# Weight blocks at other addresses and a 256/288 cut of the tokens in a one-core decoder layer

## The chip, the core and the metric

The kernel runs on one core of one Trainium2 chip. The core has a matmul engine (TensorE, "PE" in the profile, with its weight loads in a row of their own, "PEld"), a vector engine (VectorE, "DVE"), an activation engine (ScalarE, "ACT"), a general engine (GpSimd, "POOL") and a queue engine (SyncE, "SP") that issues all transfers of this kernel. They run side by side and wait for each other by semaphores. On-chip memory has 128 partitions; matmul results go to a second memory (PSUM) in banks of 512 fp32 numbers a partition. The metric is the device time of one execution in microseconds; smaller is better.

## The reference

One decoder layer, for a prompt of 512 tokens and a group of 8 x 4 sample tokens, all in fp32, model width 1024:

```python
h = _rmsnorm(x, norm_in)
proj = jnp.matmul(h, w_in)                     # 15,896 columns, split among four branches and gates
y_a = rmsnorm(ssd(...) * silu(z_ssd))          # A: Mamba-2 scan
y_b = s5(u) -> gelu -> * sigmoid(y @ glu_w) * silu(z_s5)   # B: diagonal complex SSM, 64 groups of 16
y_c = rmsnorm(sigmoid(o) * mlstm(q, k, v)) * silu(z_ml)    # C: matrix memory, 4 heads x 256
y_d = attention(q, mem_k, mem_v) * silu(z_xa)  # D: 256 memory tokens
down = jnp.einsum('btkw,kwd->btkd', branches, w_down)
merged = jnp.sum(sigmoid(gate_raw + b_gate) * down, axis=2)
x = x + jnp.matmul(merged, w_out)              # then a last RMSNorm
```

States of the three recurrent branches, and the memory's keys and values, are outputs too.

## The kernel before

The 512 prompt tokens and 32 sample tokens form one row of `NT` = 544 columns. Features lie on partitions: an activation such as h is a tile of 128 partitions by 8 row blocks (`NK`) by 544 tokens, so a row block is 544 x 4 = 2176 bytes of a partition. Each fp32 number is held as two rounded parts, hi and lo; `xh`, `xl` hold the normed input, `oh`, `ol` the current branch's output.

Nearly all projections go through one function, `unit` (line 166). It computes 128 output features for all 544 tokens: `load` fetches a 1024 x 128 block of weights (512 KB, three buffers `raw`), ACT casts it to `whi` (line 177), DVE subtracts for `wlo` (line 178, recorded at the helper's line 64), and PE runs, for each of 8 row blocks, hi x hi, hi x lo and lo x hi, each on two halves of 272 tokens (line 188): 48 matmuls, each with its own weight load of 128 x 128. `whi`, `wlo` and the result `pu` have two buffers each. In `pu` half a starts at the start of bank a. There are 165 such units; 16 further ones (`w_mem_kv`) have one part of 256 tokens, the memory's, 24 matmuls each, with token blocks of 1024 bytes. Two early units already cut at 256 and 288 (`ECUT`, line 242), because their first part starts before all tokens are there. The last product (line 1644) is written out by itself, also in parts of 288 and 256.

The work is staged: norm and transposes; cross-attention with the memory's units between; the S5 branch (lines 687 to 888); its GLU; the SSD branch; mLSTM; the last gate units; the last product. Generators such as `gate_down` are stepped between the steps of a branch, so that units fill TensorE while other engines work. The tile framework orders the instructions of each engine ahead of time by a simulated schedule: an instruction can be placed ahead of an earlier one of the program if that one still waits. On the chip each engine keeps that order.

The S5 branch runs over eight blocks f. `s5_in` runs a permuted unit, writes its result to DRAM (`ud`, line 709) and reads it back in another order into `U` (line 710, two buffers). `s5_mats` builds the block's matrices, `s5_scan` multiplies U (line 779) and scans on DVE and POOL (its first product on DVE writes `gr`, line 787), `s5_y` multiplies U a second time (line 834), and its result goes through DRAM again (`yd`, `yt`, lines 839 and 840) to `s5_out`. `s5_in` runs up to two blocks ahead. Smaller buffers that matter here: `kbt` (line 432, transposed keys of the sample group), `fo` (line 1217, a final state on its way out), `sqm` (line 1459), `yvx` (line 679).

Of the kernel before, what the change touches and what calls it, by code (L numbers as in the profile page):

```python
# [8 lines left out]
F32 = mybir.dt.float32  # L9
F32R = mybir.dt.float32r  # L10
# [6 lines left out]
P = 128  # L17
# [3 lines left out]
TS = 32  # L21
NT = TP + TS
HALF = NT // 2
NK = D // P
EPS = 1e-6
# [9 lines left out]
def hybrid_kernel(ctx: ExitStack, tc: tile.TileContext, I, O):  # L35
# [127 lines left out]
    def halves(t):  # L163
        return t.rearrange("p (a t) -> p a t", a=2)

    def unit(w, op, perm=False, raw=None, cols=HALF, nh=2, apart=False, later=False, cuts=None):

        if raw is None:
            raw = load(w)
        hi = wp.tile([P, NK, P], F32R, name="whi", tag="whi")  # L170
        lo = wp.tile([P, NK, P], F32R, name="wlo", tag="wlo")
        rv, hv, lv = raw, hi, lo
        if perm:
            rv = raw.rearrange("p k (g c) -> p k g c", c=16)
            hv = hi.rearrange("p k (c g) -> p k g c", g=8)
            lv = lo.rearrange("p k (c g) -> p k g c", g=8)
        S.copy(hv, rv)  # L177
        tt(V, lv, rv, hv.bitcast(F32), SUB)
        ps = psg.tile([P, 2, 512], F32, name="pu", tag="pu")
        xhi, xlo = op  # L180

        def part(rng):
            for k in range(NK):
                for wt, xt, first in ((hi, xhi, k == 0), (hi, xlo, False), (lo, xhi, False)):
                    last = k == NK - 1 and wt is lo
                    for a in rng:
                        c0, c1 = cuts[a] if cuts else (a * cols, (a + 1) * cols)
                        T.matmul(ps[:, a, 0:c1 - c0], wt[:, k, :], xt[:, k, c0:c1], start=first, stop=last)  # L188
        if later:
            return ps, part  # L190
        for rng in ([(a,) for a in range(nh)] if apart else (range(nh),)):
            part(rng)
        return ps
# [17 lines left out]
    def gate_down(k, first=False, ahead=2, place=None):  # L211
        gq = []

        def gate(i):
            pg = unit(wcols(C_G + k * D + i * P), x2)
            g = place(i) if place else ev.tile([P, NT], F32, name="gt", tag="gt")
            S.activation(halves(g), pg[:, :, 0:HALF], AF.Tanh, scale=0.5, bias=colh("b_gate", k * NK + i))
            gq.append(g)

        for i in range(ahead):  # L220
            gate(i)
            yield
        for i in range(NK):
            g = gq[i]
            pd = unit(I["w_down"][0, k][:, i * P:(i + 1) * P], o2)
            if first:
                stt(halves(merged[:, i, :]), halves(g), 1.0, pd[:, :, 0:HALF], ADD, MUL)
            else:
                stt(halves(g), halves(g), 1.0, pd[:, :, 0:HALF], ADD, MUL)
# [11 lines left out]
    early = []  # L241
    EC, NE, ECUT = 1, 2, ((0, 256), (256, NT))
    for c in range(5):
# [7 lines left out]
        if c < 4:  # L251
# [8 lines left out]
            if c == EC:  # L260
                for i in range(NE):
                    early.append(unit(None, x2, raw=qraw[i], later=True, cuts=ECUT))
                    early[i][1]((0,))
# [60 lines left out]
    for i in range(3):  # L324
        if i < NE:
            pu, part = early[i]
            part((1,))
            for a, (c0, c1) in enumerate(ECUT):
                S.copy(oh[:, i, c0:c1], pu[:, a, 0:c1 - c0])
                tt(V, ol[:, i, c0:c1], pu[:, a, 0:c1 - c0], oh[:, i, c0:c1].bitcast(F32), SUB)  # L330
            V.tensor_copy(qs[:, i, :], pu[:, 1, 256:288])
        else:
            pu = unit(wcols(C_QX + i * P), x2, raw=qraw[i])
            S.copy(halves(oh[:, i, :]), pu[:, :, 0:HALF])
            tt(V, halves(ol[:, i, :]), pu[:, :, 0:HALF], halves(oh[:, i, :].bitcast(F32)), SUB)
            V.tensor_copy(qs[:, i, :], pu[:, 1, 240:272])
    xmc = ExitStack()
# [25 lines left out]
    for i in range(3, NK):  # L363
        pu = unit(wcols(C_QX + i * P), x2)
        S.copy(halves(oh[:, i, :]), pu[:, :, 0:HALF])
        tt(V, halves(ol[:, i, :]), pu[:, :, 0:HALF], halves(oh[:, i, :].bitcast(F32)), SUB)
        V.tensor_copy(qs[:, i, :], pu[:, 1, 240:272])
    def mem_units():
        for i in range(16):
            pu = unit(I["w_mem_kv"][0][:, i * P:(i + 1) * P], (mh, mlo), cols=256, nh=1)  # L370
            src = xm.tile([P, 256], F32, name="vfm", tag="vfm", bufs=2)
            S.copy(src, pu[:, 0, 0:256])
            if i < 8:
# [48 lines left out]
    for b in range(NB):  # L422
# [274 lines left out]
    def s5_in(f):  # L697
# [6 lines left out]
        us = pu[:, 1, 240:272].rearrange("p (b t) -> p t b", t=4)  # L704
# [198 lines left out]
    def glu(gl):  # L903
# [4 lines left out]
        for i in range(NK):  # L908
            pg = unit(I["s5_glu_w"][0][:, i * P:(i + 1) * P], o2)
            sg = gl.tile([P, NT], F32, name="sg", tag="sg")  # L910
            S.activation(halves(sg), pg[:, :, 0:HALF], AF.Tanh, scale=0.5, bias=colh("s5_glu_b", i))
            stt(sg, sg, 1.0, zq[i], ADD, MUL)
# [6 lines left out]
    with tc.tile_pool(name="sd", bufs=1, side="right", reuse_waits="tile") as sd:  # L919
# [43 lines left out]
        def rows():  # L963
            with tc.tile_pool(name="sx", bufs=1, side="left", reuse_waits="tile") as sx:
# [9 lines left out]
                sp = sx.tile([96, NT], F32, name="sp", tag="sp")  # L974
                V.tensor_scalar(halves(X), pu[0:96, :, 0:HALF], bcol[:, 0:1], bcol[:, 1:2], ADD, MUL)
                irow = sx.tile([4, NT], F32, name="irow", tag="irow")
                S.activation(halves(irow), pu[32:36, :, 0:HALF], AF.Identity, bias=bcol[32:36, 0:1])
                yield
# [149 lines left out]
        def conv(ct):  # L1128
# [3 lines left out]
            G.memset(R[:, 0:3], 0.0)  # L1132
            S.copy(halves(R[:, 3:3 + NT]), pu[:, :, 0:HALF])
            sv = R[:, 515:571].rearrange("p (b s) -> p b s", s=7)
            V.tensor_copy(sv[:, :, 3:7], pu[:, 1, 240:272].rearrange("p (b t) -> p b t", t=4))
            V.tensor_copy(sv[:, :, 0:3], cvs[:, ct, :].rearrange("p (b t) -> p b t", t=3))
# [33 lines left out]
        for j in range(8):  # L1170
# [45 lines left out]
            T.transpose(pf[:, 0:P], SS[:, 3, :], ident)  # L1216
            fo = sr.tile([P, P], F32, name="fo", tag="fo")
            S.copy(fo, pf[:, 0:P])
# [36 lines left out]
        def ml_qkv(h, dst):  # L1255
            for t, keep, c0, sc in zip(dst, (qs, ks, vs), (C_Q, C_K, C_V), (1.0, 1.0 / 16.0, 1.0)):
                for dt in range(2):
                    pu = unit(wcols(c0 + h * 256 + dt * P), x2)
                    S.mul(halves(t[:, dt]), pu[:, :, 0:HALF], sc)
                    if dt == 0:  # L1260
# [128 lines left out]
    with tc.tile_pool(name="mlr", bufs=1, side="right", reuse_waits="tile") as mr:  # L1389
        for h in range(4):  # L1390
# [67 lines left out]
            to = mr.tile([P, 2, NT], F32, name="to", tag="to")  # L1458
            sq = mr.tile([P, TP], F32, name="sqm", tag="sqm")
            for dt in range(2):  # L1460
                pu = unit(wcols(C_O + h * 256 + dt * P), x2)
                S.activation(halves(to[:, dt]), pu[:, :, 0:HALF], AF.Tanh, scale=0.5)
                V.tensor_copy(os_[:, 2 * h + dt, :], to[:, dt, TP:NT])
# [266 lines left out]
```

## Time and profile before

| | us |
|---|---|
| median of 3 runs | 1526.18 |
| lowest and highest run | 1525.82, 1528.65 |
| the profiled execution | 1523.98 |
| its span, first to last instruction | 1522.2 |
| matmuls of line 188: busy in the span | 1121.18 |
| mean granted TensorE clock | 0.973 of full speed |

The profile is one execution on the chip. Its page gives, for each engine, the busy time, its share of the span and the count of instructions; then the span in 40 slices; then the chain of work that ended last, followed back from the last instruction. A view by stretches gives, for each stretch of the span, the busy time of PE, PEld, DVE, ACT and POOL (with counts), the granted clock, the share of time in which the DMA engines were busy, and GB/s. A timeline lists instructions by start time: start, duration, engine, line, operation, output tile <- input tiles, shapes, count of like instructions merged into the row, all in microseconds. Matmuls are pipelined: each takes some 0.28 to 0.30 us from start to end, but the next one starts long before that. What a stream of them costs is the distance between starts.

### The profile page before, as it was taken

The page shows a single profiled execution, that of the slowest core. Times are in us where ns is not written, and L with a number is a line of the kernel's source. Part 1 is how long each engine was busy: PE and PEld are TensorE (multiplying, and loading weights), DVE is VectorE, ACT ScalarE, POOL GpSimd, SP SyncE. Part 2 cuts the span into 40 slices and gives each one's busy share as a digit, 9 for nine tenths or more (in the row PEclk, how much of TensorE's full clock was granted, in tenths as well). Part 3 has the DMA queues.
Part 4 walks back from the last instruction along what each step waited for, and adds up shares of the span by engine and source line. Part 5 has one row for each costly group of instructions (what it writes and reads, how often), then busy time and mean ns, then how long its engine had stood idle before and what let it go on. Part 6 is the DMA issues. An engine that isn't in the chain of part 4 may idle for free.

```text
span 1522.2 us, 28087 instructions
## 1 busy us (share of the span) xinstructions
PE 1446.7 (95%) x11505; PEld 1364.3 (90%) x11505; DVE 925.6 (61%) x1810; ACT 485.5 (32%) x825; POOL 349.2 (23%) x527
## 2 busy tenths in 40 slices
PE   6999999789879899999999999999999999899997
PEld 6988888678768899999999989999999998789997
DVE  6355487898778768486787644354343456554543
ACT  5244333222222333243333322243332332113332
POOL 2000133766465201101232322100000011110222
PEclk9999999999789999999999999999999999999999
DMA  8577362435334333322222355222222225673341
GB/s 200 159 215 221 99 200 59 106 93 126 82 92 108 84 100 82 86 78 81 74 73 74 97 167 146 70 70 77 77 78 74 79 82 176 197 218 113 94 146 59
DMA packets 288034, 171.75 MB, mean 113 GB/s; under 512 B 36934, under 2 KB 278922, under 8 KB 287907
## 3 DMA queue, kind: packets, MB, share of 16 engines
q1 hardware_dynamic: 287906, 169.97, 40.4%
q8 instruction: 90, 1.47, 0.4%
q14 instruction: 38, 0.30, 0.1%
HBM read 145.35 MB, written 24.60 MB: 112 GB/s over the span
## 4 chain that ended last, share of the span: by engine, by line
PE 63%; DVE 10%; DMA 4%; issue 3%; POOL 2%; ACT 1%; SPq 0%; POOLq 0%; ACTq 0%; DVEq 0%
PE pu L188 48%; PE pu L1644 3%; DVE wlo L64 2%; DVE hs L64 1%; DMA raw<-in_w_out_dram 1%; DMA yd<-yj 1%; PE pacc L1557 1%; DVE bbs L752 1%; DVE cm L67 1%; PE pcu L1442 1%; DMA out_dram<-cb 1%; PE pn L1436 1%; PE py L834 1%; PE py L835 1%; DMA cb<-in_state_mlstm_c_dram 1%
## 5 line engine op out<-in xcount | busy, mean ns | idle before, releaser
L188 PE MATMUL pu<-xh,whi 128*128 128x272 f32 (+1 forms) x2000 | 432.8, 294 | 1.3 <-DVE uf L706 1.1
L188 PE MATMUL pu<-xh,wlo 128*128 128x272 f32 (+1 forms) x2000 | 428.9, 293 | 0.0
L188 PE MATMUL pu<-xl,whi 128*128 128x272 f32 (+1 forms) x2000 | 428.2, 292 | 0.6 <-DVE xl L64 0.6
L64 DVE TENSOR_TENSOR wlo<-raw,whi 128x1024 fp32r<-128x1024 f32 x181 | 251.5, 1390 | 226.3 <-ACT whi L177 221.1
L177 ACT CAST whi<-raw 128x1024 fp32r<-128x1024 f32 x181 | 198.9, 1099 | 502.6 <-PE pu L188 373.1
L188 PEld LDWEIGHTS pu<-xh,whi 128*128 128x128 f32 x2000 | 322.1, 191 | 8.3 <-issue 6.2
L188 PEld LDWEIGHTS pu<-xl,whi 128*128 128x128 f32 x2000 | 322.2, 192 | 5.6 <-issue 4.5
L188 PEld LDWEIGHTS pu<-xh,wlo 128*128 128x128 f32 x2000 | 320.2, 191 | 5.5 <-issue 5.1
L188 PE MATMUL pu<-oh,wlo 128*128 128x272 f32 x640 | 135.6, 292 | 6.0 <-DVE wlo L64 6.0
L188 PE MATMUL pu<-oh,whi 128*128 128x272 f32 x640 | 136.5, 292 | 0.0
L188 PE MATMUL pu<-ol,whi 128*128 128x272 f32 x640 | 136.4, 292 | 0.0
L188 PEld LDWEIGHTS pu<-oh,wlo 128*128 128x128 f32 x640 | 102.0, 191 | 7.7 <-DVE wlo L64 6.6
L188 PEld LDWEIGHTS pu<-ol,whi 128*128 128x128 f32 x640 | 102.7, 191 | 1.6 <-issue 1.5
L188 PEld LDWEIGHTS pu<-oh,whi 128*128 128x128 f32 x640 | 102.9, 191 | 1.0 <-issue 0.8
L64 POOL TENSOR_TENSOR merged<-merged,gt 128x544 f32<-128x544 f32 x18 | 29.1, 1616 | 142.0 <-DVE gt L67 141.9
L67 DVE SCALAR_TENSOR_TENSOR cb<-cb,dcm,pcn 128x257 f32<-128x257 f32 x64 | 28.5, 478 | 26.4 <-PE pcn L1563 26.1
L834 PE MATMUL py<-U,tp 128*128 128x72 f32 x128 | 28.3, 307 | 13.8 <-DVE hn L64 7.1
L67 DVE SCALAR_TENSOR_TENSOR cc<-cc,dcm,pcu 128x257 f32<-128x257 f32 x24 | 11.5, 478 | 44.4 <-PE pcu L1442 44.4
L188 PE MATMUL pu<-mh,whi 128*128 128x256 f32 x128 | 37.7, 294 | 0.1
L188 PE MATMUL pu<-mlo,whi 128*128 128x256 f32 x128 | 37.7, 295 | 0.0
L64 POOL TENSOR_TENSOR SS<-SS,dec 128x128 f32<-128x128 f32 x24 | 19.5, 814 | 77.6 <-DVE SS L1210 49.8
L188 PE MATMUL pu<-mh,wlo 128*128 128x256 f32 x128 | 36.2, 283 | 0.0
(641 smaller groups left out, 2297.7 us busy)
## 6 DMA issues: line engine op xcount, KB each, us to landing
raw<-in_w_in_dram SPq DMA_DIRECT2D x124, 512.0 KB
raw<-in_w_down_dram SPq DMA_DIRECT2D x32, 512.0 KB
kb<-in_cache_mem_k_dram SPq DMA_DIRECT2D x8, 1024.0 KB
raw<-in_w_mem_kv_dram SPq DMA_DIRECT2D x16, 512.0 KB
vb<-in_cache_mem_v_dram SPq DMA_DIRECT2D x16, 512.0 KB
cb<-in_state_mlstm_c_dram SPq DMA_DIRECT2D x16, 512.0 KB
out_dram<-cb SPq DMA_DIRECT2D x16, 512.0 KB
tp<-kd SPq DMA_DIRECT2D x8, 512.0 KB
```

The costliest lines, as they stand in the source:

```text
L64: eng.tensor_tensor(out, a, b, op)
L67: V.scalar_tensor_tensor(out, a, s, b, op0, op1)
L177: S.copy(hv, rv)
L188: T.matmul(ps[:, a, 0:c1 - c0], wt[:, k, :], xt[:, k, c0:c1], start=first, stop=last)
L752: V.tensor_copy(bbs[64 * ri:64 * ri + 64, :, g2, :], src[64 * g2:64 * g2 + 64, gs])
L834: T.matmul(o, tp[:, g, :], U[:, g, 0:72], start=True, stop=False)
L835: T.matmul(o, cm[:, g, 1:9, :].rearrange("p l c -> p (l c)"), hs_[:, g, 0:72], start=False, stop=True)
L1436: T.matmul(p2[:, 0:257], qh[:, dt, sl], cc[:, dt, 0:257], start=dt == 0, stop=dt == 1)
L1442: T.matmul(p3[:, 0:CE], k_[:, dt * P:(dt + 1) * P], v_, start=j == 0, stop=j == 2)
L1557: T.matmul(pacc[32 * h:32 * h + 32, 0:257], qm[:, 2 * h + dt, :], cbs_[h // 2][:, 2 * (h % 2) + dt, 0:257], start=b == 0 and dt == 0, stop ...
L1644: T.matmul(pu, wt[:, k, :], mk[:, t0:t1], start=k == 0 and j == 0, stop=k == NK - 1 and j == 2)
```

## The change

Every two-part unit now cuts the tokens at 256, so its parts have 256 and 288 columns. In `pu` the first part ends at the border of the two banks and the second begins there, so that the 544 results are one run; every reader of `pu` reads that run in place of two halves.

The weight tiles `whi` and `wlo` are larger (1128 numbers a partition in place of 1024). The even row blocks lie first, the odd ones 128 bytes further on than they would without a gap, and the matmuls take the blocks in the order 0, 2, 4, 6, 1, 3, 5, 7. The start of the `whi` part moves by 32 bytes from unit to unit, through six places; that of the `wlo` part moves every six units. Units of the memory have no gap between even and odd blocks but the same order and starts. The permuted units of S5 cast and subtract even and odd blocks separately.

To make room, `U` of the S5 branch has one buffer in place of two, `kbt` five in place of six, `fo` one in place of two; `sqm` shares the place of `Wl`, and `yvx` that of `qxs`.

```diff
+CUTS = ((0, 256), (256, NT))
+KS = (0, 2, 4, 6, 1, 3, 5, 7)
+WS = 4 * 128 + 32
...
+    turn = iter(range(1000))
...
-        hi = wp.tile([P, NK, P], F32R, name="whi", tag="whi")
-        lo = wp.tile([P, NK, P], F32R, name="wlo", tag="wlo")
-        rv, hv, lv = raw, hi, lo
+        u = next(turn)
+        hi, lo = (wp.tile([P, 2 * WS + 40], F32R, name=n, tag=n)[:, 8 * o:8 * o + 2 * WS]
+                  for n, o in (("whi", u % 6), ("wlo", (u // 6) % 6)))
+        if nh == 2:
+
+            hi, lo = (t.rearrange("p (o q) -> p o q", o=2)[:, :, 0:4 * P] for t in (hi, lo))
+        else:
+            hi, lo = (t[:, 0:NK * P].rearrange("p (o q) -> p o q", o=2) for t in (hi, lo))
+        rv = raw.rearrange("p (k o) c -> p o k c", o=2)
         if perm:
...
+            parts = [tuple(t[:, o].rearrange("p k (g c) -> p k g c", c=16) if t is rv else t[:, o].rearrange("p (k c g) -> p k g c", k=4, g=8)
+                      for t in (hi, lo, rv)) for o in range(2)]
+        else:
+            parts = [(hi.rearrange("p o (k c) -> p o k c", k=4), lo.rearrange("p o (k c) -> p o k c", k=4), rv)]
+        for hv, lv, rv in parts:
+            S.copy(hv, rv)
+            tt(V, lv, rv, hv.bitcast(F32), SUB)
...
-            for k in range(NK):
-                for wt, xt, first in ((hi, xhi, k == 0), (hi, xlo, False), (lo, xhi, False)):
-                    last = k == NK - 1 and wt is lo
+            for s, k in enumerate(KS):
+                for wt, xt, first in ((hi, xhi, s == 0), (hi, xlo, False), (lo, xhi, False)):
+                    last = s == NK - 1 and wt is lo
                     for a in rng:
-                        c0, c1 = cuts[a] if cuts else (a * cols, (a + 1) * cols)
-                        T.matmul(ps[:, a, 0:c1 - c0], wt[:, k, :], xt[:, k, c0:c1], start=first, stop=last)
+                        c0, c1 = CUTS[a]
+                        T.matmul(ps[:, a, 256 * (1 - a):256 * (1 - a) + c1 - c0], wt[:, s // 4, (s % 4) * P:(s % 4 + 1) * P],
+                                 xt[:, k, c0:c1], start=first, stop=last)
+
+        po = ps.rearrange("p a t -> p (a t)")[:, 256:256 + NT] if nh == 2 else ps[:, 0, 256:512]
...
-        S.activation(halves(z), pu[:, :, 0:HALF], AF.Tanh, scale=0.5)
-        stt(halves(z), halves(z), 1.0, pu[:, :, 0:HALF], ADD, MUL)
+        S.activation(z, pu, AF.Tanh, scale=0.5)
+        stt(z, z, 1.0, pu, ADD, MUL)
...
-            kt_ = xk.tile([P, 2, 256], F32, name="kbt", tag="kbt", bufs=6)
+            kt_ = xk.tile([P, 2, 256], F32, name="kbt", tag="kbt", bufs=5)
...
-    yv = xv.tile([P, 8, TS], F32, name="yvx", tag="yvx", bufs=1)
+    yv = xa.tile([P, 8, TS], F32, name="yvx", tag="qxs")
...
-        S.copy(uf[:, :, 8:42], pu[:, 0, 0:272].rearrange("p (k s) -> p s k", s=8))
-        S.copy(uf[:, :, 42:72], pu[:, 1, 0:240].rearrange("p (k s) -> p s k", s=8))
+        S.copy(uf[:, :, 8:72], pu[:, 0:TP].rearrange("p (k s) -> p s k", s=8))
...
-        U = s5r.tile([P, 8, NV], F32, name="U", tag="U", bufs=2)
+        U = s5r.tile([P, 8, NV], F32, name="U", tag="U", bufs=1)
...
-            fo = sr.tile([P, P], F32, name="fo", tag="fo")
+            fo = sr.tile([P, P], F32, name="fo", tag="fo", bufs=1)
...
-            sq = mr.tile([P, TP], F32, name="sqm", tag="sqm")
+            sq = mr.tile([P, TP], F32, name="sqm", tag="Wl")
```

More of the change, by code (lines that the diff above doesn't have):

```diff
@@ L160, in hybrid_kernel, with unit @@
     x2, o2 = (xh, xl), (oh, ol)
+    turn = iter(range(1000))
     ev = ctx.enter_context(tc.tile_pool(name="ev", bufs=2))
-    def halves(t):
-        return t.rearrange("p (a t) -> p a t", a=2)
-    def unit(w, op, perm=False, raw=None, cols=HALF, nh=2, apart=False, later=False, cuts=None):
+    def unit(w, op, perm=False, raw=None, nh=2, later=False):
         if raw is None:
             raw = load(w)
-        hi = wp.tile([P, NK, P], F32R, name="whi", tag="whi")
-        lo = wp.tile([P, NK, P], F32R, name="wlo", tag="wlo")
-        rv, hv, lv = raw, hi, lo
-        if perm:
[L174 to L178, printed above, removed]
+        u = next(turn)
[6 more added lines that the diff above has]
+        rv = raw.rearrange("p (k o) c -> p o k c", o=2)
+        if perm:
+            parts = [tuple(t[:, o].rearrange("p k (g c) -> p k g c", c=16) if t is rv else t[:, o].rearrange("p (k c g) -> p k g c", k=4, g=8)
[5 more added lines that the diff above has]
+            tt(V, lv, rv, hv.bitcast(F32), SUB)
         ps = psg.tile([P, 2, 512], F32, name="pu", tag="pu")
@@ L182, in part @@
         def part(rng):
-            for k in range(NK):
-                for wt, xt, first in ((hi, xhi, k == 0), (hi, xlo, False), (lo, xhi, False)):
-                    last = k == NK - 1 and wt is lo
+            for s, k in enumerate(KS):
+                for wt, xt, first in ((hi, xhi, s == 0), (hi, xlo, False), (lo, xhi, False)):
+                    last = s == NK - 1 and wt is lo
                     for a in rng:
-                        c0, c1 = cuts[a] if cuts else (a * cols, (a + 1) * cols)
-                        T.matmul(ps[:, a, 0:c1 - c0], wt[:, k, :], xt[:, k, c0:c1], start=first, stop=last)
+                        c0, c1 = CUTS[a]
+                        T.matmul(ps[:, a, 256 * (1 - a):256 * (1 - a) + c1 - c0], wt[:, s // 4, (s % 4) * P:(s % 4 + 1) * P],
+                                 xt[:, k, c0:c1], start=first, stop=last)
+        po = ps.rearrange("p a t -> p (a t)")[:, 256:256 + NT] if nh == 2 else ps[:, 0, 256:512]
         if later:
[L190 to L193, printed above, removed]
+            return po, part
+        part(range(nh))
+        return po
     def zgate(pool, c0, tag="zz", bufs=None):
@@ L261, in hybrid_kernel @@
                 for i in range(NE):
-                    early.append(unit(None, x2, raw=qraw[i], later=True, cuts=ECUT))
+                    early.append(unit(None, x2, raw=qraw[i], later=True))
                     early[i][1]((0,))
@@ L327, in hybrid_kernel @@
             part((1,))
[L328 to L331, printed above, removed]
+            for a, (c0, c1) in enumerate(CUTS):
+                S.copy(oh[:, i, c0:c1], pu[:, c0:c1])
+                tt(V, ol[:, i, c0:c1], pu[:, c0:c1], oh[:, i, c0:c1].bitcast(F32), SUB)
+            V.tensor_copy(qs[:, i, :], pu[:, TP:NT])
         else:
             pu = unit(wcols(C_QX + i * P), x2, raw=qraw[i])
-            S.copy(halves(oh[:, i, :]), pu[:, :, 0:HALF])
-            tt(V, halves(ol[:, i, :]), pu[:, :, 0:HALF], halves(oh[:, i, :].bitcast(F32)), SUB)
-            V.tensor_copy(qs[:, i, :], pu[:, 1, 240:272])
+            S.copy(oh[:, i, :], pu)
+            tt(V, ol[:, i, :], pu, oh[:, i, :].bitcast(F32), SUB)
+            V.tensor_copy(qs[:, i, :], pu[:, TP:NT])
     xmc = ExitStack()
@@ L364, in hybrid_kernel @@
         pu = unit(wcols(C_QX + i * P), x2)
-        S.copy(halves(oh[:, i, :]), pu[:, :, 0:HALF])
-        tt(V, halves(ol[:, i, :]), pu[:, :, 0:HALF], halves(oh[:, i, :].bitcast(F32)), SUB)
-        V.tensor_copy(qs[:, i, :], pu[:, 1, 240:272])
+        S.copy(oh[:, i, :], pu)
+        tt(V, ol[:, i, :], pu, oh[:, i, :].bitcast(F32), SUB)
+        V.tensor_copy(qs[:, i, :], pu[:, TP:NT])
     def mem_units():
         for i in range(16):
-            pu = unit(I["w_mem_kv"][0][:, i * P:(i + 1) * P], (mh, mlo), cols=256, nh=1)
+            pu = unit(I["w_mem_kv"][0][:, i * P:(i + 1) * P], (mh, mlo), nh=1)
             src = xm.tile([P, 256], F32, name="vfm", tag="vfm", bufs=2)
-            S.copy(src, pu[:, 0, 0:256])
+            S.copy(src, pu)
             if i < 8:
@@ L910, in glu @@
             sg = gl.tile([P, NT], F32, name="sg", tag="sg")
[L911 removed]
+            S.activation(sg, pg, AF.Tanh, scale=0.5, bias=colh("s5_glu_b", i))
             stt(sg, sg, 1.0, zq[i], ADD, MUL)
@@ L1258, in ml_qkv @@
                     pu = unit(wcols(c0 + h * 256 + dt * P), x2)
-                    S.mul(halves(t[:, dt]), pu[:, :, 0:HALF], sc)
+                    S.mul(t[:, dt], pu, sc)
                     if dt == 0:
```

20 lines of the change are left out of this document (10 added, 10 removed).

## The prediction

> **What bounds the kernel now.** I read the page from the top, then the stages of the unit's matmuls (line 188), then single stretches of the timeline. The page first:
>
> ```profile
> span 1522.2 us, 28087 instructions
> PE 1446.7 (95%) x11505; PEld 1364.3 (90%) x11505; DVE 925.6 (61%) x1810; ACT 485.5 (32%) x825; POOL 349.2 (23%) x527
> ...
> PE 63%; DVE 10%; DMA 4%; issue 3%; POOL 2%; ACT 1%; SPq 0%; POOLq 0%; ACTq 0%; DVEq 0%
> PE pu L188 48%; PE pu L1644 3%; DVE wlo L64 2%; DVE hs L64 1%; DMA raw<-in_w_out_dram 1%; DMA yd<-yj 1%; PE pacc L1557 1%; DVE bbs L752 1%; DVE cm L67 1%; PE pcu L1442 1%; DMA out_dram<-cb 1%; PE pn L1436 1%; PE py L834 1%; PE py L835 1%; DMA cb<-in_state_mlstm_c_dram 1%
> ```
>
> TensorE is busy 95% of the span and holds 63% of the chain that ended last; the projections' matmuls of line 188 alone hold 48%. So the spacing of those matmuls decides, in every stage but one. The views by stretches, first of everything in the S5 stage, then of line 188 over all stages, show the exception:
>
> ```profile
> 235.00:530.00 295.00, 249.18 (x1998) 227.78 (x1991) 242.66 (x476) 81.43 (x141) 151.95 (x230) 0.91 0.40 96
> ```
>
> ```profile
> 235.00:530.00 295.00, 172.88 (x1193) 163.07 (x1194) 0.91 0.40 96
> ...
> sum 1522.20, PE 1121.18 PEld 1072.37; mean PE 140.15 PEld 134.05
> ```
>
> In the 295 us of the S5 stage PE is idle for 46 us, DVE is busy for 243, and the granted clock is 0.91: a recurrence of small steps on DVE, POOL and DMA sets the time there. Only 1193 of line 188's 8304 matmuls (14%) lie in it.
>
> **The change part by part.**
>
> *The cut of the tokens.* There are 181 units: 16 of the memory with one part of 256 columns, unchanged, and 165 with two parts, 24 pairs of matmuls each, 3960 pairs. A pair was 272 + 272 columns and becomes 256 + 288. The trace has all three widths in steady streams. The bars of single matmuls overlap, so I take distances between starts (timeline, PE alone). 272 columns, in the GLU stage:
>
> ```profile
> 600.12 0.42 PE L188 MATMUL pu<-xh,whi 128*128 128x272 f32 x2
> ...
> 602.38 0.41 PE L188 MATMUL pu<-xh,whi 128*128 128x272 f32 x2
> ```
>
> Nine pairs in 2.26 us: 251.1 ns a pair. 256 columns, in a unit of the memory, and 288 columns, in the two units that already cut at 256:
>
> ```profile
> 120.08 0.29 PE L188 MATMUL pu<-mh,whi 128*128 128x256 f32 x1
> ...
> 121.39 0.28 PE L188 MATMUL pu<-mh,wlo 128*128 128x256 f32 x1
> ```
>
> ```profile
> 33.21 0.29 PE L188 MATMUL pu<-xl,whi 128*128 128x288 f32 x1
> ...
> 36.14 0.29 PE L188 MATMUL pu<-xh,wlo 128*128 128x288 f32 x1
> ```
>
> Eleven steps in 1.31 us are 119.1 ns, 22 steps in 2.93 us are 133.2 ns; the new pair would be 252.3 ns, 1.2 more than the old. The final product (line 1644) has the same two widths with its weights at other places:
>
> ```profile
> 1470.94 0.43 PE L1644 MATMUL pu<-mh,wxl 128*128 128x288 f32 x2
> ...
> 1473.33 0.42 PE L1644 MATMUL pu<-mh,wxl 128*128 128x288 f32 x2
> ...
> 1497.82 0.40 PE L1644 MATMUL pu<-mh,wxl 128*128 128x256 f32 x2
> ...
> 1500.19 0.28 PE L1644 MATMUL pu<-mlo,wxl 128*128 128x256 f32 x1
> ...
> 1503.96 0.40 PE L1644 MATMUL pu<-mh,woh 128*128 128x256 f32 x2
> ...
> 1505.01 0.40 PE L1644 MATMUL pu<-mh,woh 128*128 128x256 f32 x2
> ```
>
> 18 steps in 2.39 us (132.8 ns), 20 in 2.37 us (118.5 ns), and, at its fastest, nine in 1.05 us (116.7 ns). So the pair lies between 116.7 + 132.8 = 249.5 and 252.3 ns, that is 1.6 below to 1.2 above the old. I take +0.8, between the two streams' 251.3 and 252.3 and nearer the units' own. Without the S5 stage's 14% some 3400 pairs are on the path: **+2.7 us, between -5.4 and +4.1**.
>
> *The places of the weights.* No instruction is added: a unit still issues 48 matmuls and 48 weight loads of the same shape. What changes is the distance in bytes between the token block that streams and the weight block that is loaded meanwhile. Tokens step by 544 x 4 = 2176 bytes a row block, 8.5 times 256; weights step by 512. So before, the distance (mod 256) flips by 128 with each block; the change moves odd blocks 128 on, takes the even ones first and cuts at byte 1024, so that within a unit it stays the same for the hi part and for the lo part, at values that walk in 32-byte steps from unit to unit. Do distances matter here? The units of the memory are a test: their tokens step by 1024 bytes and their weights by 512, so their distance never flips, and they run at 119.1 ns against the final product's 118.5 where it does flip. Constant distance alone bought nothing there; stretches of the final product with other pairs of blocks differ by 1.8 ns (118.5 against 116.7). I put this at nothing beyond the bounds above.
> [...]
>
> *Reading the result.* The two parts now lie side by side over the border of two banks and are read as one run of 544 instead of two of 272: same elements, same count of instructions, nothing. The permuted S5 units cast and subtract in two halves: 8 units, each one more ACT and one more DVE instruction. A full-size subtract takes 1.23 us (row below); as halves I estimate 0.1 to 0.2 us more from the fixed part, 8 x 0.15 = **+1 us** of DVE at most, less the S5 input's two copies becoming one.
>
> *The smaller buffers.*
>
> ```profile
> L64 DVE TENSOR_TENSOR wlo<-raw,whi x181: 1157/1226/2960, 13.8 to 1447.6; 128x1024 fp32r<-128x1024 f32 x181
> ```
>
> ```profile
> 70.00:235.00 165.00, 164.87 (x1310) 138.93 (x1308) 99.35 (x253) 60.06 (x116) 34.40 (x67) 1.00 0.58 173
> ```
>
> ```profile
> L61 DVE COPY kbt<-pkt x16: 684/691/693, 83.2 to 161.1; 128x512 f32<-128x512 f32 x16
> ...
> L1218 ACT COPY fo<-pfin x8: 248/261/266, 703.5 to 857.4; 128x128 f32<-128x128 f32 x8
> ```
>
> `fo` with one buffer: its eight copies are (857.4 - 703.5) / 7 = 22 us apart, and each output transfer has that long to land. `kbt` with five: PE is busy for 164.87 of that stage's 165 us (first row), and only the second to fourth copies of the next sequence wait; 0 to 1 us. `sqm` in `Wl`'s place and `yvx` in `qxs`'s follow the last reader by several us: nothing.
>
> *One S5 input block.* This is the one added wait. U of block f+1 may be fetched only when `s5_y` of block f has read the old U (line 834). It then takes an issue on SP and a read back from DRAM; after it line 779's 32 matmuls, and then DVE's first product, `gr`. Prices: the chain has two fetches of this kind.
>
> ```profile
> 347.01 6.87 DMA yd<-yj
> ...
> 491.99 3.85 DMA yt<-yd
> ```
>
> The read back took 3.85 us (U is 320 KB, `yt` 288 KB). With 0.33 us of issue and some 1.3 us of matmuls, `gr` can start 5.5 us after the last matmul of `s5_y`. What stands there now, at the last two hand-overs and at one of the five before, of which it is the shortest (each time the last matmuls of `s5_y`, then DVE's `gr`):
>
> ```profile
> 345.43 0.28 PE L835 MATMUL py<-hs,cm 128*128 128x72 f32 x1
> ...
> 352.86 0.41 DVE L64 TENSOR_TENSOR gr<-st,pvr 128x256 f32<-128x256 f32 x1
> ```
>
> ```profile
> 485.67 0.39 PE L835 MATMUL py<-hs,cm 128*128 128x72 f32 x2
> ...
> 488.81 0.42 DVE L64 TENSOR_TENSOR gr<-st,pvr 128x256 f32<-128x256 f32 x1
> ```
>
> ```profile
> 508.39 0.39 PE L835 MATMUL py<-hs,cm 128*128 128x72 f32 x2
> ...
> 509.98 0.42 DVE L64 TENSOR_TENSOR gr<-st,pvr 128x256 f32<-128x256 f32 x1 [0.36 <-PE pvi L779]
> ```
>
> In five of seven DVE comes to `gr` 7 us or more after `s5_y` ended, behind the next block's matrices: the fetch hides there. The last two (2.7 and 1.2 us) would be 2.8 and 4.3 us late, 7 us if nothing fills them; PE has gate units and DVE their weights to do. I take **+2, between 0 and 7**, with U's fetch ahead of `yd` on SP's queue. Queued behind the waiting U are the next weights' loads, three deep, and nothing else urgent.
>
> Sum: 2.7 + 0.5 + 2 = about +5 us. The profiled execution took 1523.98 us (1.8 around its span), 2.2 below the median of 1526.18; on the median the forecast is **1531 us**, its own range 1524 to 1538.
>
> **The rivals.**
> *Placement pays (faster).* Single spacings do get shorter than the mean, in the first units:
>
> ```profile
> 20.36 0.28 PE L188 MATMUL pu<-xh,wlo 128*128 128x256 f32 x1
> 20.48 0.28 PE L188 MATMUL pu<-xh,whi 128*128 128x256 f32 x1
> 20.59 0.28 PE L188 MATMUL pu<-xl,whi 128*128 128x256 f32 x1
> 20.71 0.28 PE L188 MATMUL pu<-xh,wlo 128*128 128x256 f32 x1
> ```
>
> 0.12, then 0.11, then 0.12 us; this short one follows an odd row block's first matmul. If a fixed distance makes one matmul in three that short, a pair falls by 9 x 2/3 = 6 ns, 3400 pairs by 20 us; with the cut and U back, **1511** (1495 to 1523). For it: spacing varies with the block at all. Against: the memory's units, always at one distance, average 119.1. It decides from 1.4 ns a pair on.
> *No change.* Distances give back the 0.8 ns of the cut and U hides wholly: 1526, within 1523 to 1529. This is also the case in which the change doesn't do what its layout says, because varying starts average over good and bad distances.
> *U comes late (slower).* If its fetch stands behind `yt`'s on SP, which waits 6.87 us for `yd` to land, `gr` comes 12.8 us after `s5_y`; the shown and similar gaps then lack 6, 6, 10 and 11.5 us, some 30 in all, and PE, with more idle time, may see the lower clock more often than the stage's 0.91 shows now. Half filled: **1545**, up to 1562.
>
> **How the numbers follow.** Forecast 0.40, placement pays 0.27, no change 0.18, U late 0.15. About 0.2% (3 us) is what a measurement of this kernel can tell from no change: below 1523.1 or above 1529.2. The forecast's own range lies about 0.29 above that line, 0.10 inside and 0.01 below. So faster 0.28, same 0.28, slower 0.44. The range reaches from 1505 to 1548: it cuts the far parts of the first rival and of U late, about 0.15.
>
> **What would show it.** Distances between starts in a middle stage: 252 ns a pair for the forecast, under 249 if placement pays; and units that differ among themselves by their start. The S5 stage (235 to 530) keeps its 295 us within 5, and DVE's wait for line 779 at the last two blocks shows U; a stage 15 us longer would mean U is late. ACT's and DVE's reads of `pu` keep their durations. I am wrong if the pair moves by more than 2 ns either way, which no row above shows for any placement.

## The result and the profile after

| | before | after |
|---|---|---|
| median, us (18 runs each, side by side) | 1524.33 | 1533.91 |
| lowest and highest, us | 1519.05, 1528.65 | 1527.18, 1539.04 |
| ratio, 95% interval | | 1.0062 (1.0050 to 1.0075) |

The change makes the kernel 0.62% slower, about 9.5 us. The profiled execution after took 1527.18 us, the quickest of its 18 and the one with the highest mean granted clock (0.974; the others have 0.965 to 0.973), so its trace shows only part of the loss. The page of after, first its span and busy times, then its chain by engine and by line:

```profile
span 1525.5 us, 28112 instructions
PE 1448.6 (95%) x11505; PEld 1368.6 (90%) x11505; DVE 928.7 (61%) x1818; ACT 486.1 (32%) x825; POOL 353.4 (23%) x527
...
PE 63%; DVE 10%; DMA 6%; issue 2%; ACT 1%; POOL 1%; SPq 0%; POOLq 0%; ACTq 0%; DVEq 0%
PE pu L197 48%; PE pu L1654 2%; DVE wlo L67 2%; PE py L844 1%; PE py L845 1%; DMA raw<-in_w_out_dram 1%; DMA yd<-yj 1%; DVE cm L70 1%; PE pacc L1567 1%; DMA out_dram<-cb 1%; PE pcu L1452 1%; DVE hs L67 1%; PE pn L1446 1%; DVE t L67 1%; POOL q L67 1%
```

The counts on PE are those of before, the share of the unit's matmuls (now line 197) is the same; only DMA holds more of the chain (6% against 4%). Where the time went shows when the span is cut at the last matmul of `s5_y`, which moved from 530.20 to 541.10. View by stretches, everything: PE, PEld, DVE, ACT and POOL busy, then granted clock, DMA share, GB/s. Before, then after:

```profile
235.00:530.20 295.20, 249.38 (x1999) 227.97 (x1992) 242.66 (x476) 81.43 (x141) 151.95 (x230) 0.91 0.40 96
530.20:1522.00 991.80, 975.51 (x7792) 942.29 (x7790) 547.78 (x1025) 314.77 (x521) 151.83 (x197) 0.99 0.36 103
```

```profile
235.00:541.10 306.10, 260.07 (x2052) 240.72 (x2045) 247.10 (x487) 83.33 (x143) 157.25 (x230) 0.90 0.40 94
541.10:1525.50 984.40, 967.69 (x7743) 934.68 (x7742) 546.32 (x1022) 313.37 (x519) 150.95 (x197) 0.99 0.36 103
```

The S5 stage is 10.9 us longer and the rest 7.4 us shorter. PE's idle time in the stage is the same (295.20 - 249.38 = 45.8 us, 306.10 - 260.07 = 46.0): what is added is busy time. 53 more matmuls lie in the stage, 49 fewer behind it; at 125 ns each, 6 to 7 us of unit work were only moved forward. The rest is loss.

The pace of the unit hardly changed. The same view of PE alone, over 64 us of the last gate units, where PE never pauses (the count is the number of matmuls; two of them are not the unit's). Before, then after:

```profile
1384.00:1448.00 64.00, 64.00 (x515) 1.00 0.32 91
```

```profile
1387.00:1451.00 64.00, 64.00 (x514) 1.00 0.31 91
```

Over the whole trace a pair takes 250.6 ns before and 250.2 after. This figure, used below for each run, is the mean distance between starts from the first part to the second plus that from the second to the first (some 3600 of each, without pauses over 150 ns and without stretches at a granted clock of 0.5).

The last hand-over of U shows the new wait. SP's queue of after, then the chain of waits in the same stretch (start, length, what):

```profile
510.13 0.63 SPq L779 DMA_DIRECT2D tp<-kd  x1
510.85 6.08 SPq L946 DMA_DIRECT2D raw<-in_w_in_dram  x3
517.04 0.52 SPq L720 DMA_DIRECT2D U<-ud  x1
517.60 0.43 SPq L849 DMA_DIRECT2D yd<-yj  x1
```

```profile
513.14 0.22 PE py L845 x2
513.36 3.68 PE pu L197 x29
517.04 3.58 DMA U<-ud
520.62 0.04 issue
520.67 0.61 PE pvr L789 x4
521.28 0.24 PE pvi L789 x4
```

`s5_y` ends at 513.36; U's fetch goes out 3.7 us later, because three loads of small weight columns (line 946) hold SP for 6.08 us; then 3.58 us of read back, and matmuls at a granted clock of 0.50 (520.5 to 522.9; 0.24 us for four, mostly 0.12 in the block before, at 1.00). DVE's `gr` starts 9.5 us after `s5_y`, where it was 1.2 before, and DVE waits 3.57 us for it, where it was 0.36:

```profile
522.90 0.42 DVE L67 TENSOR_TENSOR gr<-st,pvr 128x256 f32<-128x256 f32 x1 [3.57 <-PE pvr L789]
```

### The profile page after: what moved, and what is told of

Read it like the earlier page. It is cut to its first block, busy times and chain, and to the rows that moved or that the text cites. A ratio compares the mean times of both kernels' runs of the same rounds, so it can differ in the third digit from the quotient of the medians.

```text
span 1525.5 us, 28112 instructions
## 1 busy us (share of the span) xinstructions
PE 1448.6 (95%) x11505; PEld 1368.6 (90%) x11505; DVE 928.7 (61%) x1818; ACT 486.1 (32%) x825; POOL 353.4 (23%) x527
## 4 chain that ended last, share of the span: by engine, by line
PE 63%; DVE 10%; DMA 6%; issue 2%; ACT 1%; POOL 1%; SPq 0%; POOLq 0%; ACTq 0%; DVEq 0%
PE pu L197 48%; PE pu L1654 2%; DVE wlo L67 2%; PE py L844 1%; PE py L845 1%; DMA raw<-in_w_out_dram 1%; DMA yd<-yj 1%; DVE cm L70 1%; PE pacc L1567 1%; DMA out_dram<-cb 1%; PE pcu L1452 1%; DVE hs L67 1%; PE pn L1446 1%; DVE t L67 1%; POOL q L67 1%
## 5 line engine op out<-in xcount | busy, mean ns | idle before, releaser
L197 PE MATMUL pu<-xh,whi 128*128 128x256 f32 x2000 | 431.4, 294 | 3.7 <-DVE zz L70 1.8
L197 PE MATMUL pu<-xl,whi 128*128 128x256 f32 x2000 | 429.3, 292 | 0.6 <-DVE xl L67 0.6
L197 PE MATMUL pu<-xh,wlo 128*128 128x256 f32 x2000 | 427.9, 293 | 0.0
L67 DVE TENSOR_TENSOR wlo<-raw,whi 128x1024 fp32r<-128x1024 f32 (+1 forms) x189 | 253.1, 1341 | 228.0 <-ACT whi L186 218.4
L186 ACT CAST whi<-raw 128x1024 fp32r<-128x1024 f32 (+1 forms) x189 | 198.6, 1061 | 497.4 <-PE pu L197 384.5
L197 PEld LDWEIGHTS pu<-xh,wlo 128*128 128x128 f32 x2000 | 327.0, 191 | 6.0 <-issue 5.6
L197 PE MATMUL pu<-oh,wlo 128*128 128x256 f32 (+1 forms) x640 | 136.8, 294 | 0.8 <-DVE wlo L67 0.8
L197 PE MATMUL pu<-oh,whi 128*128 128x256 f32 (+1 forms) x640 | 137.5, 295 | 0.0
L197 PE MATMUL pu<-ol,whi 128*128 128x256 f32 (+1 forms) x640 | 137.1, 293 | 0.0
L844 PE MATMUL py<-U,tp 128*128 128x72 f32 x128 | 31.0, 333 | 18.7 <-DVE hn L67 12.6
L844 PEld LDWEIGHTS py<-U,tp 128*128 128x128 f32 x128 | 25.2, 244 | 19.6 <-DVE hn L67 12.9
L70 DVE SCALAR_TENSOR_TENSOR cc<-cc,dcm,pcu 128x257 f32<-128x257 f32 x24 | 11.5, 477 | 44.4 <-PE pcu L1452 44.4
```

The costliest lines, as they stand in the source:

```text
L67: eng.tensor_tensor(out, a, b, op)
L70: V.scalar_tensor_tensor(out, a, s, b, op0, op1)
L197: T.matmul(ps[:, a, 256 * (1 - a):256 * (1 - a) + c1 - c0], wt[:, s // 4, (s % 4) * P:(s % 4 + 1) * P], xt[:, k, c0:c1], start=first, stop ...
L844: T.matmul(o, tp[:, g, :], U[:, g, 0:72], start=True, stop=False)
```

## The experiments

All ratios are to the kernel before, run beside each, with a 95% interval; 0.1% is 1.5 us.

**U with one block, nothing else.**

```diff
-        U = s5r.tile([P, 8, NV], F32, name="U", tag="U", bufs=2)
+        U = s5r.tile([P, 8, NV], F32, name="U", tag="U", bufs=1)
```

> The kernel before with one U block and nothing else of the change. Theory (from the two traces, where the last matmuls of line 779 come 12.8 us and the last of s5_y 10.9 us later after the change, while the start of the first scan is equal): the one block is the whole of that, so this kernel is 8 to 13 us slower than before, about 1534 on the median of 1524, and its last matmul on U comes 10 to 13 us later than 509.9. Rival (the prediction's price): +2, between 0 and 7; then the rest of the S5 stage's delay comes from the cut, the split casts or the placement.

Measured: 1.0083 (1.0058 to 1.0108), 12.6 us. In its trace the last of line 779's matmuls starts at 530.4, 20 us later than before and not the 10 to 13 expected. DVE's last `gr`, then the view by stretches:

```profile
530.67 0.42 DVE L64 TENSOR_TENSOR gr<-st,pvr 128x256 f32<-128x256 f32 x1 [4.27 <-PE pvr L779]
```

```profile
235.00:548.90 313.90, 265.83 (x2055) 246.58 (x2048) 244.65 (x480) 85.06 (x144) 154.50 (x230) 0.87 0.38 92
548.90:1537.00 988.10, 968.36 (x7736) 934.63 (x7735) 544.52 (x1021) 312.01 (x518) 150.83 (x197) 0.99 0.35 102
```

The one block costs more than the whole change. It hardly adds idle time in the stage (48.1 us against 45.8), but the granted clock falls from 0.91 to 0.87. In the traces of before and after every clock entry is 1.0 or 0.5 of full speed. If this trace holds no others, the time at 0.5 is 2 x (1 - clock) x length, an estimate from the rows: 82 us here, 53 before, where the entries themselves add up to 54.6. Over both stretches PE is busy 9.3 us longer (16.45 more in the stage, 7.15 less behind it) for the same matmuls, and idle 5.7 us longer (2.25 and 3.45). So some 60% of the price in this execution is slower matmuls, not waiting. The times of the six executions point the same way: two took 1528.70 and 1530.44 us at a mean granted clock of 0.971, four took 1537.06 to 1538.72 at 0.964 to 0.968.

**The small loads moved behind U's last fetch.**

```diff
...
-        dma(U, ud.rearrange("q (c g) k -> (q c) g k", g=8))
+        udma.append(dma(U, ud.rearrange("q (c g) k -> (q c) g k", g=8)).ins)
...
+        with tc.issue_after(udma[7]):
+            for d0, c0, n in ((0, C_DT, 16), (32, C_I, 4), (64, C_F, 4)):
+                dma(raw[:, :, d0:d0 + n], I["w_in"][0][:, c0:c0 + n].rearrange("(k p) c -> p k c", p=P))
```

> The kernel before with one U block, and the three small column loads of line 936 kept behind U's last fetch on SP's queue. In the run with one U block alone that fetch was issued 4.8 us after the last matmul of s5_y (519.8 to 524.6), behind these loads. Theory (the queue's part of the price is real): the last fetch goes out right behind s5_y, some 4 us of the 12.6 come back, a ratio of about 1.0055. Rival (the end of S5 is covered by later units): 1.008 as without it.

Measured: 1.0054 (1.0034 to 1.0074). SP's queue of this run:

```profile
512.11 0.63 SPq L769 DMA_DIRECT2D tp<-kd  x1
514.59 0.33 SPq L710 DMA_DIRECT2D U<-ud  x1
514.98 0.43 SPq L938 DMA_DIRECT2D raw<-in_w_in_dram  x1
515.45 1.15 SPq L839 DMA_DIRECT2D yd<-yj  x1
516.64 3.82 SPq L938 DMA_DIRECT2D raw<-in_w_in_dram  x2
```

The fetch goes out as `s5_y` ends, and the median falls by 0.29%, as the queue theory had it. The two intervals overlap, and the two quickest executions of U alone (1528.70 and 1530.44) were as quick without this edit, so the rows show the fetch go out earlier, but the runs do not show what that is worth. The matmuls on U still start only 6.1 us after the fetch (520.71), 1.49 us of them PE's wait for it; after the change it was 3.63 us (517.04 to 520.67). The loads and the write of `yd` now go out in that time; whether they make it longer is not shown.

**U freed earlier.** The eight matmuls of `s5_y` that read U come first, the eight that wait for the scan behind them (each of them counts as two in the rows).

```diff
+        pys = [bank("py") for _ in range(2)]
+        for g in range(8):
+            T.matmul(pys[g // 4][:, (g % 4) * 72:(g % 4 + 1) * 72], tp[:, g, :], U[:, g, 0:72], start=g % 4 == 0, stop=False)
         for hb in range(2):
...
-                T.matmul(o, tp[:, g, :], U[:, g, 0:72], start=True, stop=False)
```

> The kernel before with one U block, but in s5_y the eight matmuls that read U come first and the eight that wait for the scan behind them, so U is free earlier at each hand-over. Theory (the wait for U is the price of 12.6 us that the run with one U block alone showed): U's fetch goes out 2 us or more earlier, and at least half of the price comes back, a ratio of 1.001 to 1.005 to the kernel before. Rival (the price comes from the other order of the units that the planner makes, not from the wait): stays at 1.008.

Measured: 1.0128 (1.0102 to 1.0154), slower than without the edit. Neither theory foresaw that. A hand-over in the middle, SP's queue and PE:

```profile
381.27 0.52 SPq L710 DMA_DIRECT2D U<-ud  x1
```

```profile
380.82 3.62 PE L836 MATMUL py<-hs,cm 128*128 128x72 f32 x16
384.18 0.57 PE L188 MATMUL pu<-oh,wlo 128*128 128x272 f32 x1
...
390.45 0.41 PE L188 MATMUL pu<-oh,wlo 128*128 128x272 f32 x2
390.79 0.35 PE L779 MATMUL pvr<-U,bt 128*64 128x72 f32 x4
```

U's fetch is out 2.9 us before `s5_y` ends, yet line 779 starts 9.5 us after the fetch: the rest of a gate unit stands ahead of it in PE's order, without a pause and, in its first rows, at 0.45 us for two matmuls (384.56 to 385.01) where the later ones take 0.25 (388.45 to 388.70). The order was fixed ahead of time, and an earlier fetch changes nothing in it. At the last hand-over the early end is lost on the queue, and DVE waits twice as long as with the one block alone:

```profile
515.13 1.98 PE L831 MATMUL py<-U,tp 128*128 128x72 f32 x16
```

```profile
516.97 6.03 SPq L938 DMA_DIRECT2D raw<-in_w_in_dram  x3
523.11 0.51 SPq L710 DMA_DIRECT2D U<-ud  x1
```

```profile
528.68 0.42 DVE L64 TENSOR_TENSOR gr<-st,pvr 128x256 f32<-128x256 f32 x1 [8.96 <-PE pvr L779]
```

The last reads of U end at 517.1, but the small loads hold SP until 523.0. The whole of the loss against the one block alone isn't settled: the order that the framework plans ahead by its simulated schedule (the planner) differs throughout, and the edit takes both result banks at once.

**The cut alone.** Parts of 256 and 288, read as one run; weights and all buffers as before.

```diff
-                        c0, c1 = cuts[a] if cuts else (a * cols, (a + 1) * cols)
-                        T.matmul(ps[:, a, 0:c1 - c0], wt[:, k, :], xt[:, k, c0:c1], start=first, stop=last)
+                        c0, c1 = CUTS[a]
+                        T.matmul(ps[:, a, 256 * (1 - a):256 * (1 - a) + c1 - c0], wt[:, k, :],
+                                 xt[:, k, c0:c1], start=first, stop=last)
```

> The kernel before with parts of 256 and 288 columns read as one run of 544; weights, their order and all buffers as before. Theory (from the spacing of starts in the two traces, 250.6 ns a pair before and about 250.2 after): the cut costs nothing, 0.4 ns a pair less or the same, so 0 to 3 us faster. Rival (the prediction): +0.8 ns a pair, +2.7 us, at most +4.1.

Measured: 0.9967 (0.9951 to 0.9984), 5 us faster, more than the 0 to 3 expected; 249.8 ns a pair, 0.8 less than before. Times 3960 pairs that is 3.2 of the 5 us; the interval, 2.4 to 7.5 us, has room for either.

**Fixed starts.** The changed kernel, with two settings of the starts; all five engines issue the same instructions in the same order as in the changed kernel, only addresses differ. The first added line is `start_best`, the second `start_worst`:

```diff
-                  for n, o in (("whi", u % 6), ("wlo", (u // 6) % 6)))
+                  for n, o in (("whi", 3 * (u % 2)), ("wlo", 2 + 3 * (u % 2))))
+                  for n, o in (("whi", 3 * (u % 2)), ("wlo", 5 - 5 * (u % 2))))
```

> The changed kernel with fixed starts: the tokens lie 128 (mod 256) bytes from the hi block and 0 from the lo block in every unit, the pair of distances whose units were the quickest in the changed kernel's trace (248.4 ns a pair in nine units, against 250.2 over all). Theory (the distance sets the spacing): 1.8 ns a pair, 3400 pairs, 6 us faster than the changed kernel, about 1528. Rival (what else ran beside those nine units made them quick): as the changed kernel within 2 us, pairs of 250.2.

> The changed kernel with fixed starts at distances 128 (hi) and 160 (lo), ten units of which took 251.0 ns a pair in the changed kernel's trace. Theory (the distance sets the spacing): 0.8 ns a pair, 3 us slower than the changed kernel and 9 us slower than the run with 128 and 0. Rival (the distance has no part in it): equal to that run within 2 us.

Measured: 1.0027 (1.0013 to 1.0041) and 1.0089 (1.0070 to 1.0108), with the changed kernel between them; 248.3 and 250.6 ns a pair. In 64 us of the last gate units, the better, then the worse starts:

```profile
1384.00:1448.00 64.00, 64.00 (x518) 1.00 0.31 92
```

```profile
1398.00:1462.00 64.00, 64.00 (x514) 1.00 0.32 91
```

3960 pairs x 2.3 ns are 9.1 us; the medians are 9.6 apart (1526.73, 1536.35). With one program order and two address maps nothing else is left: the places of the weights do count. Which property of the places it is, this pair of runs can't tell.

**Four corners of the layout.** To have two U blocks and the better distances, `whi` and `wlo` share one tile of 2112 numbers (the scratch columns `wr`, `wi` make the room). The main lines of `best_u2` against the changed kernel; without the gap `g` is `4 * P`, and in natural order `KS` is `tuple(range(8))` and the block is found by `k`:

```diff
...
+        wt2 = wp.tile([P, 2112], F32R, name="wu", tag="wu")
+        g = WS if nh == 2 else 4 * P
+        hi, lo = (bass.AP(tensor=t.tensor, offset=t.offset, ap=[list(t.ap[0]), [g, 2], [1, 4 * P]])
+                  for t in (wt2[:, 0:1056], wt2[:, 1056:2112]))
...
-        U = s5r.tile([P, 8, NV], F32, name="U", tag="U", bufs=1)
+        U = s5r.tile([P, 8, NV], F32, name="U", tag="U", bufs=2)
```

> The cut at 256, odd blocks 128 bytes on and last, hi at distance 128 and lo at 0 in every unit (both parts in one tile of 8448 bytes, so that both buffers have the same places), and two U blocks again; two small S5 set-up columns share a scratch row to make the room. Theory (cut, placement and U add up): the run with the cut alone stood at 0.9967; the placement takes 1.4 ns from its 249.8 a pair, 3400 pairs, 4.8 us more: 0.9935, about 1512.5 of 1522.3. Rival (fixed starts gave their gain only against the worse starts): as the cut alone, 0.9967.

> As the run with fixed starts and two U blocks, but the matmuls take the row blocks in their natural order 0 to 7; every distance is the same as there. Theory (only the distance of a matmul to the weights loaded beside it counts): equal to that run within 2 us. Rival (taking odd blocks last has a part in it, since with alternating blocks the weights being loaded belong to the other half at each block's border): 2 to 5 us slower.

> The best run's kernel without the 128 bytes between even and odd blocks, still even blocks first and odd blocks last: the even half of each unit keeps the distances 128 (hi) and 0 (lo), the odd half has 0 and 128; the instructions stand in the same order on TensorE. It is the fourth corner beside the best run (gap and order, 0.9951), the run in natural order with the gap (0.9993) and the cut alone (neither, 0.9967). Theory (the distance decides, so half of each unit loses the gain): 249.2 to 249.8 ns a pair and 0.998 to 0.9995 by the time, 4 to 7 us slower than the best run. Rival (taking the odd blocks last carries the gain by itself, the gap nothing): equal to the best run, 0.995.

> The best run's kernel with plain weights in natural order: no 128 bytes between even and odd blocks and blocks 0 to 7 in turn, so the distances flip between 0 and 128 with each block as they did before the change. With the best run (gap and order, 0.9951), the one with the gap alone (0.9993) and the one with the order alone (1.0016) it completes four corners of one kernel. Theory (gap and order pay together only, because the weights loaded beside a matmul are then at the right distance too): 249.5 to 250.2 ns a pair, 0.9985 to 1.001, so the pair of edits is worth 5 to 9 us. Rival (this kernel's plain form is as quick as the cut alone, 0.9967, and the odd corners are the ones that lose): 0.996 to 0.9975.

| odd blocks | gap 128 bytes | ns a pair | ratio |
|---|---|---|---|
| in turn | no (`neither`) | 251.3 | 1.0029 (1.0016 to 1.0042) |
| last | no (`order_only`) | 250.2 | 1.0016 (1.0005 to 1.0028) |
| in turn | yes (`best_nat`) | 249.4 | 0.9993 (0.9980 to 1.0006) |
| last | yes (`best_u2`) | 248.4 | 0.9951 (0.9934 to 0.9967) |

The first and the last corner in 64 us of the last gate units:

```profile
1383.00:1447.00 64.00, 64.00 (x511) 1.00 0.32 92
```

```profile
1376.00:1440.00 64.00, 64.00 (x518) 1.00 0.34 96
```

From the first corner to the last the time follows the pace: 2.9 ns x 3960 = 11.5 us, measured 0.78%, 11.9. The two rows with the odd blocks last have the same instructions in the same order on every engine, and so have the two in turn; within each of these pairs only addresses differ, and the gap brings 1.8 and 1.9 ns. The order of the blocks brings 1.0 to 1.1 with or without the gap, so order counts although each matmul's distance to its own weights is the same.

The expectations missed in four ways. `best_u2` has the pace expected but stands at 0.9951 and not at 0.9935. `best_nat` is slower than `best_u2` by more than its rival's 2 to 5 us (6.4), `order_only` by more than its theory's 4 to 7 (9.9), and the plain corner is beyond its 249.5 to 250.2 ns. Gap and order do not pay only together: by the pace they add up. By the time they need not: one edit alone brings 5.5 (gap) and 2.0 us (order), which leaves 4.4 of the 11.9 unexplained, with intervals of about 2 us on either side of each ratio. And the plain corner is slower than the cut alone, which also takes blocks in turn without a gap but has hi and lo at equal distances and in two tiles. So the cut's own gain holds for one placement, not for another.

**All buffers back, and two tiles again.**

`best_full` gives `kbt`, `fo`, `sqm` and `yvx` their room of before; `best_two` does that too and takes a tile for each part, with the odd blocks in front in every second buffer. One line that `best_full` gives back, then the tiles of `best_two` against `best_full`:

```diff
-            kt_ = xk.tile([P, 2, 256], F32, name="kbt", tag="kbt", bufs=5)
+            kt_ = xk.tile([P, 2, 256], F32, name="kbt", tag="kbt", bufs=6)
...
-        wt2 = wp.tile([P, 2112], F32R, name="wu", tag="wu")
+        hi, lo = (wp.tile([P, 1056], F32R, name=n, tag=n) for n in ("whi", "wlo"))
```

> The best run's kernel with the smaller buffers given back: six transposed key buffers, two for the final state, own places for sqm and yvx. All engines issue the same instructions in the same order as there. Theory (the prediction's: these buffers cost 0 to 1 us): 0.9945 to 0.996, within 2 us of the best run. Rival (sqm in Wl's place or the fifth key buffer makes waits that the planner did not see): 3 to 5 us faster, 0.9925 or less.

> The cut, odd blocks 128 bytes on and last, hi at distance 128 and lo at 0 in every unit, two U blocks and all buffers as before, now with whi and wlo in tiles of their own (1056 numbers; in every second buffer the odd blocks lie in front, so that the places are the same). The four corners with one tile for both lie on a line of about 1.0 ns a pair to 4 us, but the cut alone, with two tiles at 249.8 a pair, stands 5 to 6 us below that line. Theory (one tile for both parts costs those 5 to 6 us, since both are only freed together): 248.4 a pair and 0.991 to 0.9935, about 1511. Rival (the cut alone was lucky in its order, two tiles bring nothing): 0.995 to 0.9965, as the best run.

Measured: 0.9960 (0.9947 to 0.9973) and 0.9946 (0.9926 to 0.9966). The smaller buffers cost nothing that can be seen. Two tiles are not shown to be better than one; the interval leaves both theories room, and whether the cut alone stood low by its order of work stays open. Both, like `best_u2`, beat the kernels before and after: about 0.5% below before. `start_best` and `best_two` have the same distances and the same 248.3 ns a pair and differ in U, in the small buffers and in where the tiles lie: 1.0027 against 0.9946, 0.8%, close to U's price of 0.83%.

## Why the prediction was right in sum and wrong in its terms

The forecast of 1531 us, "slower" as the likeliest, stands 3 us below the median, but two of its terms missed in opposite directions: the cut by -7.7 us, U by +10.6. That the sum came out so near is luck, helped by the base: it was 1526.18 from three runs, against 1524.33 beside the changed kernel, so the forecast change of +5 stands against a measured one of about 9.5.

*What bounds the kernel:* right. PE's busy time and the unit's share of the chain did not move, and S5 was the exception that decided.

*The cut (+2.7, between -5.4 and +4.1):* the sign was wrong; alone it is -5.0 (-2.4 to -7.5 by its interval). The step that failed took 119.1 and 133.2 ns from streams of a single width and added them. In the alternating stream of the run with the cut alone the two steps take 118.0 and 131.8, over some 3600 steps each. The lower bound, from other rows (249.5 a pair), was the nearer one. Alternating is not the reason by itself: the corner without gap and order alternates too and takes 117.9 and 133.5, 251.3 a pair. So the size hangs on the placement too, which the text took for nothing.

*The places (0):* the sum came out about right, the reason did not. The walking starts average good and bad places: after has 250.2 a pair against the cut's 249.8, 1.4 us, and what is left of the change once U (0.83%) and the cut (-0.33%) are taken off is 0.12%, 1.8 us, which the intervals do not tell from nothing. That was the "no change" rival's sentence on averaging. But "the memory's units, always at one distance, average 119.1" compared one distance with another kernel part; it could not tell distances from each other. Fixed starts span 248.3 to 250.6 with identical work. The rival that placement pays had the direction, with 6 ns a pair where at most 2.9 were found. The units of the changed kernel did differ by their start, as the text said they should if this were so: by pair of starts the means run from 248.4 (128 and 0 bytes, nine units) to 251.6 (128 and 192, five units).
The fixed starts are 0.6% apart with nothing changed but addresses, so the runs speak against placement being worth nothing; what it is in the addresses that counts, they do not show.

*Reading the result and the split casts:* as predicted. ACT's gate read takes 710 ns (708 before), DVE's 722 (721); the subtracts for `wlo` take 253.1 us of DVE in place of 251.5, 1.6 more against the +1 estimated, 0.2 for each of the eight units against the author's 0.15. (A permuted one took not 1.23 us but 2.23 before the change, at 315.19 in the rows below.)

*The smaller buffers (0 to 1):* right.

*One U block (+2, between 0 and 7):* the direction and the queue were right: U goes out ahead of `yd` (517.04, 517.60 above), not behind `yt`, so the rival with its 30 us is out. The size was wrong: 12.6 (8.8 to 16.4 by its interval). The wait that the text priced is there, and of about the size that it gave: DVE waits for the matmuls on U (line 789, before the change 779) at the last hand-over alone, 3.57 us after the change and 4.27 with U alone, against 0.36 before. What the step left out are four things.

First, the order. "The fetch hides" behind DVE's gap of 7 us took that gap as given, but the planner fills the stretch with other work, and `gr` comes later even where DVE does not wait. After block 0, before and then after the change:

```profile
315.19 2.23 DVE L64 TENSOR_TENSOR wlo<-raw,whi 128x1024 fp32r<-128x1024 f32 x1
317.33 0.67 DVE L64 TENSOR_TENSOR bm<-bm,q 128x512 f32<-128x512 f32 x1
317.93 0.40 DVE L64 TENSOR_TENSOR gr<-st,pvr 128x256 f32<-128x256 f32 x1
```

```profile
317.84 1.60 DVE L67 TENSOR_TENSOR q<-pwi,cti 128x576 f32<-128x576 f32 x1
319.54 2.25 DVE L67 TENSOR_TENSOR cm<-q,q 64x576 f32<-64x576 f32 x2
321.82 0.42 DVE L67 TENSOR_TENSOR gr<-st,pvr 128x256 f32<-128x256 f32 x1
```

`s5_y` ends at 310.9 before and at 309.8 after, so 7.1 us became 12.0; `q` and `cm`, which came behind `gr`, now stand ahead of it. Over all seven hand-overs the time from `s5_y` to `gr` grew from 61.7 to 77.9 us. How much of that is lost and how much is work only moved, the runs do not separate. Second, the queue: the text named what stands behind U on SP, "nothing else urgent", but not the 6.08 us of small loads ahead of it; the median was 0.29% lower with them moved, with the doubt said above. Third, "PE has gate units to do": it did them, and its idle time in the stage hardly grew, but a unit that the planner has put ahead of line 779 delays the recurrence to the unit's end, as the middle hand-over with U freed earlier shows. Fourth, the clock, which the text gave only to the rival: 0.87 against 0.91 in the stage with U alone, 9.3 us of slower matmuls in that execution, the largest part there. The rival tied the lower clock to more idle time of PE; that was the author's estimate, and the stage with U alone has 48.1 us of it against 45.8. What sets the clock is not shown. It came in stretches: 17.1 us of the run with U alone stand at 0.51, the next 10.2 at 0.99 (PE alone):

```profile
447.70:464.80 17.10, 11.45 (x52) 0.51 0.40 103
464.80:475.00 10.20, 9.67 (x104) 0.99 0.50 129
```

*What would show it:* "the S5 stage keeps its 295 us within 5" was wrong by 6 us; the pair at 250.2 lies between the forecast's 252 and the rival's 249. A shift of more than 2 ns, "which no row above shows for any placement", did not come with the walking starts, but fixed ones are 2.3 ns apart.

## What to carry to other kernels

A double buffer on a recurrent path is priced from the end of the last read to the next use, with whatever stands ahead of the fetch on its queue and ahead of its user on the engine, and with the granted clock of the stage; here the bare latency was only the lower end. The layout that walks through places showed next to nothing in sum (250.2 ns a pair against the cut's 249.8): fix the place, run the best and the worst of it with the same instruction order, and only then judge. A forecast near the median proves none of its terms; runs of the single edits do.

## What the runs showed of the hardware

In these runs TensorE's spacing changed with the addresses alone: 248.3 against 250.6 ns a pair, 0.9%, with the same instructions in the same order (`start_best`, `start_worst`). With the order of the blocks changed too it was 248.4 against 251.3, 1.2% (`best_u2`, `neither`). In `best_u2` the steps from a 256-column matmul on `wlo` weights, at distance 0 (mod 256 bytes, a modulus that the author chose and no run varies) both from its own weights and from those loaded next, have a median of 113 ns; in `best_nat`, at the same addresses with the blocks in turn, 119 (some 1200 steps each). So in these two the distance alone does not decide, and what does is not settled here. Three loads of 16, 4 and 4 columns of the weights hold SP for 6.08 us, as the row of line 946 shows; the load of a whole block of 128 columns a little earlier, on the same queue of after:

```profile
486.73 0.36 SPq L85 DMA_DIRECT2D raw<-in_w_in_dram  x1
```

So in this trace the time on the queue did not follow the size. Nor was it the same for the same loads: moved behind U's fetch, the first of the three took 0.43 us and the other two 3.82 together. What sets it isn't shown.
